# Seven block products for two of eight pairs of tiles in the values, the gates and both output projections, and a later first such pair in w2

## The chip, the cores and the metric

The kernel runs on one core of a Trainium2 chip. The metric is the device time of one execution in microseconds (us); the kernel before has a median of 1559.32 us over 3 runs (1559.26 to 1560.52). Five engines work side by side, each through its own list of instructions in order: TensorE (PE, matrix products), VectorE (DVE), ScalarE (ACT), GpSimd (POOL) and SyncE (SP, which issues the transfers from memory).

## The reference

One decoder layer on 256 tokens of width 2048, in fp32. Matrices that the change touches: the three column groups of `w_in` that give values and gates, `w_out`, and `xo`, all multiplied by a 256-row operand, and `w2`, whose plan alone changes.

```python
proj = x @ w_in[l]
q_m, k_m, v_m, o_m, i_m, f_m, q_a, k_a, v_a = split_columns(proj, IN_SPLITS)
y_m = mlstm_mixer(q_m, k_m, v_m, o_m, i_m, f_m, conv_w[l], conv_b[l], gate_b[l], mh_g[l])
y_a = dilated_attention(q_a, k_a, v_a, rel_bias)
x = layer_norm(ALPHA * x + concat(y_m, y_a) @ w_out[l], ln_g[l, 0], ln_b[l, 0])
y = memory_cross_attention(x, mem, xq[l], xk[l], xv[l], xo[l])      # ends in o @ xo
x = layer_norm(ALPHA * x + y, ln_g[l, 1], ln_b[l, 1])
x = layer_norm(ALPHA * x + (silu(x @ w1[l]) * (x @ w3[l])) @ w2[l], ln_g[l, 2], ln_b[l, 2])
```

## The kernel before

**Split products.** TensorE multiplies fp32r numbers. To keep fp32 accuracy every operand is kept as a high and a low part, and each product of tiles is three matmuls: high by high, high by low, low by high. A matmul takes a 128x128 stationary tile of the operand and 512 columns of the weights.

**The way of the weights.** Weights come from memory as raw tiles `w` of 1 MB, which hold a *pair* of k-tiles (two times 128 rows, 1024 columns); a ring of 3 such tiles (RAW). ACT casts a k-tile to its high part (`h`), DVE subtracts it from the raw tile to get the low part (`l`); a ring of 5 such couples (SPLIT). Then PE uses both.

**The plain product** (`gemm_tokens`) goes through 8 pairs, that is 16 k-tiles, for 2 halves of 128 rows and 2 column halves: 16 x 2 x 2 x 3 = 192 matmuls into 4 banks of PSUM. The values `v0`, `v1`, the gates `v2`, the halves of the first output projection `wo0`, `wo1` and of the second one `xo0`, `xo1` are done so, `f0` too. After `v0` and `v1`, `rows_of` copies the 4 banks to SBUF (2 copies on ACT, 2 on DVE); after `v2` ACT takes the tanh straight from the banks; after the projections `Norm.add` scales the residual `z` and adds the banks.

**The product with sevens** (`gemm_seven`) is used before for the groups `f2` to `f20` of the feed-forward block and for `w2` (`w2a0`, `w2a1`, `w2b0`, `w2b1`). A plan lists the pairs; one in brackets is a *seven*: its 2x2 blocks (two k-tiles, two column halves, two row halves) are multiplied in a scheme of seven block products `P1`, `P2`, `P3`, `Q4`, `P5`, `P7`, `Q6` in place of eight, so 21 matmuls in place of 24. For it, `sums` adds the raw weights on DVE (L308, one instruction over 128x1024, L312 and L313 over 128x512), and the weights, the sums included, are split in one piece of 512 and three of 1024 columns. The operand's tiles must be mixed too (`mix_again`: L152, four adds L141 to L144, and a split). The results lie in 5 banks of the pool `pg` (P1, P2, P3, Q4, E) and 3 of the pool `ps` (P5, P7, Q6), which is all of PSUM; once the last seven is done, `early` combines P1, P5, P7 and Q6 with `z` (`into_z`, 1 copy on ACT and 7 instructions on DVE) or with rows in SBUF (`into_rows`, 1 copy and 4 instructions); when the last plain pair is done the other four banks are added.

**The order.** Each engine's list is laid out ahead by a scheduler that simulates the kernel; so instructions of one stage stand among those of others. Around `v1` DVE's list has the convolution of the queries and keys (L583, L588, L594) and the attention (L495 to L506); around `w2a0` the end of `f10`, whose products of the gate (silu on ACT L953, products on DVE L954) are turned by PE (L959, tile `f10p`) and split into `hT`; after `xo1` the second normalization (L663, L713 to L731), whose rows PE turns for `f0` (L742, tile `x2p`). `xo1` keeps its last 6 k-tiles (LAG) in SBUF and does their products with the second row half at the end, so that the first row half can go through the normalization meanwhile.

Of the kernel before, what the change touches and what calls it, by code (L numbers as in the profile page):

```python
# [50 lines left out]
def decoder_layer(ctx: ExitStack, tc: tile.TileContext, A):  # L51
# [360 lines left out]

    def rows_of(banks, name):
        out = []
        for m in range(2):
            out.append([slot(f"{name}{m}{c}") for c in range(2)])
            for c in range(2):
                (SC.copy if c else V.tensor_copy)(out[m][c], banks[m][c])
        return out

    def turned(rows, j, name):
# [692 lines left out]
```

## Time and profile before

| | us |
|---|---|
| median of 3 runs | 1559.32 |
| the profiled execution's own time | 1558.89 |
| its span in the trace | 1557.0 |
| PE busy | 1533.5 |
| DVE busy | 1097.5 |
| ACT busy | 753.0 |

The span is the time from the first to the last instruction of the trace. Busy times of PE come from modelled ends of pipelined matmuls. The engine letters are those of the first section; PEclk is the clock that was granted to TensorE in a stretch, as a share of the full 2.4 GHz.

### The profile page before, as it was taken

To read this page: it belongs to the slowest core of one execution; us is meant where nothing else is said; L and a number is where in the kernel's file an instruction comes from. 1 tells how busy PE (TensorE), PEld (TensorE's weight loads), DVE (VectorE), ACT (ScalarE), POOL (GpSimd) and SP (SyncE) were. 2 spreads that over 40 slices of the span, in tenths; PEclk is the share of its full clock that TensorE was granted. 3 is DMA by queue.
4 is the path that set the end of the run, shared out by engine and by line. 5 is a ranking of instruction groups with operands and counts; after the bars stand their busy time and mean duration, and the time that the engine had idled before them with its cause. 6 is when DMAs were issued, how large, how long until landed. Compare 5 with 4: busy or idle time off the path is not lost.

```text
span 1557.0 us, 19142 instructions
## 1 busy us (share of the span) xinstructions
PE 1533.5 (98%) x7452; PEld 1284.9 (83%) x7452; DVE 1097.5 (70%) x1426; ACT 753.0 (48%) x974; POOL 28.3 (2%) x30
## 2 busy tenths in 40 slices
PE   9999999999999999999998999999899999999997
PEld 7888888888888888888887888887788888888885
DVE  6555774586557655555559678887788778888997
ACT  5445554454433544444434554555446455555551
POOL 0000000000000000000004000000000000000000
PEclk9999999999999999999999999999999999999999
DMA  8664455575554555445553465665465656667552
GB/s 300 238 237 176 150 196 190 185 263 184 200 193 163 201 187 196 180 139 192 188 189 135 163 214 192 216 193 191 147 222 177 205 189 192 214 192 258 199 189 108
DMA packets 83352, 301.33 MB, mean 194 GB/s; under 512 B 7181, under 2 KB 9402, under 8 KB 59710
## 3 DMA queue, kind: packets, MB, share of 16 engines
q1 hardware_dynamic: 83262, 300.12, 56.0%
q8 instruction: 58, 0.95, 0.2%
q14 instruction: 32, 0.26, 0.1%
HBM read 297.97 MB, written 4.21 MB: 194 GB/s over the span
## 4 chain that ended last, share of the span: by engine, by line
PE 96%; DVE 3%; DMA 1%; issue 0%; ACT 0%; SPq 0%; DVEq 0%; ACTq 0%
PE w2a0P L338 2%; PE w2a1P L338 2%; PE w2b0P L338 2%; PE w2b1P L338 2%; PE f10P L338 2%; PE f18P L338 1%; PE f16P L338 1%; PE f14P L338 1%; PE f20P L338 1%; PE f8P L338 1%; PE f12P L338 1%; PE f2P L338 1%; PE f6P L338 1%; PE f4P L338 1%; PE w2a0Q L338 1%; PE w2a1Q L338 1%
## 5 line engine op out<-in xcount | busy, mean ns | idle before, releaser
L257 DVE TENSOR_TENSOR v2l<-v2w,v2h 128x1024 fp32r<-128x1024 f32 x16 | 19.6, 1225 | 21.9 <-ACT v2h L256 21.9
L257 DVE TENSOR_TENSOR v0l<-v0w,v0h 128x1024 fp32r<-128x1024 f32 x16 | 19.6, 1226 | 21.7 <-ACT v0h L256 21.6
L257 DVE TENSOR_TENSOR xv1l<-xv1w,xv1h 128x1024 fp32r<-128x1024 f32 x16 | 19.6, 1225 | 20.7 <-ACT xv1h L256 20.6
L257 DVE TENSOR_TENSOR xv0l<-xv0w,xv0h 128x1024 fp32r<-128x1024 f32 x16 | 19.6, 1226 | 19.9 <-ACT xv0h L256 19.9
L257 DVE TENSOR_TENSOR wo0l<-wo0w,wo0h 128x1024 fp32r<-128x1024 f32 x16 | 19.6, 1226 | 18.7 <-ACT wo0h L256 18.5
L110 ACT CAST w2a1h<-w2a1w 128x1024 fp32r<-128x1024 f32 (+1 forms) x24 | 22.8, 981 | 20.4 <-PE w2a1E L338 11.8
L257 DVE TENSOR_TENSOR xo0l<-xo0w,xo0h 128x1024 fp32r<-128x1024 f32 x16 | 19.6, 1225 | 18.4 <-ACT xo0h L256 18.4
L257 DVE TENSOR_TENSOR wo1l<-wo1w,wo1h 128x1024 fp32r<-128x1024 f32 x16 | 19.4, 1223 | 17.9 <-ACT wo1h L256 17.7
L110 ACT CAST w2a0h<-w2a0w 128x1024 fp32r<-128x1024 f32 (+1 forms) x24 | 22.7, 979 | 16.8 <-PE w2a0E L338 8.2
L256 ACT CAST wo1h<-wo1w 128x1024 fp32r<-128x1024 f32 x16 | 16.8, 1055 | 26.7 <-PE wo1b L276 18.4
L256 ACT CAST f0h<-f0w 128x512 fp32r<-128x512 f32 (+1 forms) x22 | 16.8, 813 | 26.5 <-PE xo1b L276 14.5
L256 ACT CAST v2h<-v2w 128x1024 fp32r<-128x1024 f32 x16 | 16.9, 1055 | 25.2 <-PE v2b L276 18.5
L257 DVE TENSOR_TENSOR v1l<-v1w,v1h 128x1024 fp32r<-128x1024 f32 x16 | 19.6, 1223 | 13.1 <-ACT v1h L256 13.1
L256 ACT CAST v0h<-v0w 128x1024 fp32r<-128x1024 f32 x16 | 16.9, 1054 | 24.6 <-PE v0b L276 19.4
L256 ACT CAST xv1h<-xv1w 128x1024 fp32r<-128x1024 f32 x16 | 16.9, 1055 | 23.8 <-PE xv1b L276 17.2
L111 DVE TENSOR_TENSOR w2a1l<-w2a1w,w2a1h 128x1024 fp32r<-128x1024 f32 (+1 forms) x24 | 26.5, 1130 | 2.5 <-ACT w2a1h L110 2.5
L110 ACT CAST w2b0h<-w2b0w 128x1024 fp32r<-128x1024 f32 (+1 forms) x20 | 19.2, 988 | 17.0 <-PE w2b0E L338 10.1
L256 ACT CAST xv0h<-xv0w 128x1024 fp32r<-128x1024 f32 x16 | 16.9, 1054 | 21.6 <-PE xv0b L276 16.4
L256 ACT CAST wo0h<-wo0w 128x1024 fp32r<-128x1024 f32 x16 | 16.9, 1054 | 21.3 <-PE wo0b L276 15.0
L111 DVE TENSOR_TENSOR w2a0l<-w2a0w,w2a0h 128x1024 fp32r<-128x1024 f32 (+1 forms) x24 | 26.4, 1129 | 0.9 <-ACT w2a0h L110 0.9
L338 PE MATMUL w2a0P<-w2a0h,hT 128*128 128x512 f32 x80 | 26.8, 395 | 0.0
L256 ACT CAST xo0h<-xo0w 128x1024 fp32r<-128x1024 f32 x16 | 16.8, 1051 | 20.4 <-PE xo0b L276 16.2
(1388 smaller groups left out, 5431.6 us busy)
## 6 DMA issues: line engine op xcount, KB each, us to landing
w2a0w<-in_w SPq DMA_DIRECT2D x12, 1024.0 KB, 5.0
w2a1w<-in_w SPq DMA_DIRECT2D x12, 1024.0 KB, 4.9
w2b0w<-in_w SPq DMA_DIRECT2D x10, 1024.0 KB, 5.0
w2b1w<-in_w SPq DMA_DIRECT2D x10, 1024.0 KB, 4.9
v0w<-in_w_v SPq DMA_DIRECT2D x8, 1024.0 KB, 5.1
v1w<-in_w_v SPq DMA_DIRECT2D x8, 1024.0 KB, 4.9
v2w<-in_w_v SPq DMA_DIRECT2D x8, 1024.0 KB, 4.9
wo0w<-in_w_out SPq DMA_DIRECT2D x8, 1024.0 KB, 4.9
```

The costliest lines, as they stand in the source:

```text
L110: SC.copy(hi, src)
L111: V.tensor_tensor(out=lo, in0=src, in1=as_f32(hi), op=ALU.subtract)
L256: SC.copy(wh[:, cs], w[:, i, cs])
L257: eng.tensor_tensor(out=wl[:, cs], in0=w[:, i, cs], in1=as_f32(wh[:, cs]), op=ALU.subtract)
L338: T.matmul(of[to], lhsT, rhs, start=to not in begun, stop=end)
```

## The change

`v0`, `v1`, `v2`, `wo0`, `wo1`, `xo0` and `xo1` go from `gemm_tokens` to `gemm_seven`, each with 2 sevens among its 8 pairs; operand pairs 2 and 5 of `xT`, 5 and 7 of `yT`, 1 and 3 of `oT` are mixed once for it. `rows_of` is gone; `whole` (4 adds on DVE) adds the last banks to the rows of `into_rows`, and the tanh of the gates reads those rows. The plan of `w2a0` and `w2a1` keeps its four sevens (pairs 2, 4, 6, 8), but three plain pairs stand ahead of the first one where one did.

```diff
-    def rows_of(banks, name):
...
-                (SC.copy if c else V.tensor_copy)(out[m][c], banks[m][c])
+    def whole(rows, banks):
+        for m in range(2):
+            for c in range(2):
+                V.tensor_tensor(out=rows[m][c], in0=rows[m][c], in1=banks[m][c], op=ALU.add)
...
     def in_rows(i):
-        return gemm_tokens(xT, A["w_v"][i], KT, f"v{i}")
+        rows, plan = [], [0, 1, (2,), 3, 4, (5,), 6, 7]
+        if not xT.mixed:
+            xT.mix_again(2)
+            xT.mix_again(5)
+        banks = gemm_seven(xT, fetch(A["w_v"][i], f"v{i}"), KT, f"v{i}", plan, into_rows(rows, f"v{i}r"))
+        whole(rows, banks)
+        return rows
...
-    va = rows_of(in_rows(0), "va")
+    va = in_rows(0)
...
-    vm = rows_of(in_rows(1), "vm")
+    vm = in_rows(1)
...
-    banks = in_rows(2)
+    gate = in_rows(2)
...
-            SC.activation(t, banks[m][c], ACT.Tanh, scale=0.5)
+            t = gate[m][c]
+            SC.activation(t, t, ACT.Tanh, scale=0.5)
...
+    for j in (5, 7):
+        yT.mix_again(j)
     for g in range(2):
-        banks = gemm_tokens(yT, A["w_out"][g], KT, f"wo{g}", order, last=g == 1)
+        get, plan = fetch(A["w_out"][g], f"wo{g}"), [0, 2, (1,), 4, 5, (3,), 6, 7]
+        banks = gemm_seven(yT, get, KT, f"wo{g}", plan, into_z(g, ALPHA), order, last=g == 1)
         for m in range(2):
-            ln.add(m, g, banks, stats=False)
+            ln.add(m, g, banks, stats=False, scale=1.0)
...
-    banks = gemm_tokens(oT, A["xo"][0], KT, "xo0")
+    for j in (1, 3):
+        oT.mix_again(j)
+    plan = [0, 2, (1,), 4, (3,), 5, 6, 7]
+    banks = gemm_seven(oT, fetch(A["xo"][0], "xo0"), KT, "xo0", plan, into_z(0, ALPHA))
...
-    banks = gemm_tokens(oT, A["xo"][1], KT, "xo1", kept=range(KT - LAG, KT), last=True)
+    plan, kept = [0, (1,), 2, (3,), 4, 5, 6, 7], range(KT - LAG, KT)
+    banks = gemm_seven(oT, fetch(A["xo"][1], "xo1"), KT, "xo1", plan, into_z(1, ALPHA), None, kept, True)
...
     def w2_first():
-        plan = [0, (2,), 1, (4,), 3, (6,), 5, (8,), 7, 9, 10, 11]
+        plan = [0, 1, 3, (2,), 5, (4,), 7, (6,), 9, (8,), 10, 11]
```

In the lists of instructions that follow, the number behind a name's letters is that of its pair or k-tile, and the one behind the underscore tells tiles of one name apart.

DVE's list before, where `f10` ends and `w2a0` begins: the products of `f10`'s gate (L954), the split of `hT` from the turned tile `f10p`, and the sums of the first two sevens, pairs 2 and 4.

```order
L954 TENSOR_TENSOR f10ru_8795<-f10ru_8795,f10r00_8796 128x256
L954 TENSOR_TENSOR f10r11_8798<-f10r11_8798,f10r00_8796 128x256
L954 TENSOR_TENSOR f10r01_8797<-f10r01_8797 128x256
L111 TENSOR_TENSOR hT10_8887<-f10p0_8882,hT10_8887 128x2x256
L308 TENSOR_TENSOR w2a0t2_8947<-w2a0w2_8945 128x1024
L308 TENSOR_TENSOR w2a0t4_9025<-w2a0w4_9023 128x1024
L111 TENSOR_TENSOR hT11_8900<-f10p1_8895,hT11_8900 128x2x256
L312 TENSOR_TENSOR w2a0s2_8948<-w2a0t2_8947,w2a0w2_8945 128x512
```

The same place of DVE's list now (the gate's products are at L962):

```order
L111 TENSOR_TENSOR w2a0l6_9261<-w2a0w3_9258,w2a0h6_9260 128x1024
L962 TENSOR_TENSOR f10ru_9074<-f10ru_9074,f10r00_9075 128x256
L962 TENSOR_TENSOR f10r11_9077<-f10r11_9077,f10r00_9075 128x256
L111 TENSOR_TENSOR w2a0l7_9277<-w2a0w3_9258,w2a0h7_9276 128x1024
L111 TENSOR_TENSOR w2a0l2_9300<-w2a0w2_9292,w2a0h2_9299 128x512
L962 TENSOR_TENSOR f10r01_9076<-f10r01_9076 128x256
L111 TENSOR_TENSOR hT10_9166<-f10p0_9161,hT10_9166 128x2x256
L111 TENSOR_TENSOR w2a0l2_9307<-w2a0w2_9292,w2a0h2_9306 128x1024
L308 TENSOR_TENSOR w2a0t2_9294<-w2a0w2_9292 128x1024
L308 TENSOR_TENSOR w2a0t4_9372<-w2a0w4_9370 128x1024
L111 TENSOR_TENSOR hT11_9179<-f10p1_9174,hT11_9179 128x2x256
L312 TENSOR_TENSOR w2a0s2_9295<-w2a0t2_9294,w2a0w2_9292 128x512
```

The splits of pair 3 (and ahead of these, those of pair 1) now stand among the gate's products; the sums still follow the last of these products, and PE has three plain pairs to do ahead of the first seven.

DVE's list before in the middle of `v1`, at the end of the convolution (L588, L594) and the start of an attention head (L495):

```order
L257 TENSOR_TENSOR v1l5_1946<-v1w2_1927,v1h5_1945 128x1024
L588 SCALAR_TENSOR_TENSOR k0_1842<-q0_1639,cw_535,k0_1842 128x254
L257 TENSOR_TENSOR v1l6_1964<-v1w3_1961,v1h6_1963 128x1024
L594 SCALAR_TENSOR_TENSOR i5r1_1828<-i5r1_1828,i4r1_1625 128x512
L588 SCALAR_TENSOR_TENSOR k0_1842<-q0_1639,cw_535,k0_1842 128x253
L257 TENSOR_TENSOR v1l7_1980<-v1w3_1961,v1h7_1979 128x1024
L495 SCALAR_TENSOR_TENSOR i2r0_1088<-sc7_1425,tb4_523 128x384
```

The same place of DVE's list now (the convolution's lines are L580 and L586, the head's is L487); `v1l2` are the weights of the first seven, pair 2, and `v1l6` those of the k-tile that follows it:

```order
L111 TENSOR_TENSOR v1l2_1993<-v1w2_1978,v1h2_1992 128x1024
L580 SCALAR_TENSOR_TENSOR k0_1889<-q0_1686,cw_535,k0_1889 128x253
L111 TENSOR_TENSOR v1l2_2003<-v1t2_1980,v1h2_2002 128x1024
L586 SCALAR_TENSOR_TENSOR i5r1_1875<-i5r1_1875,i4r1_1672 128x512
L111 TENSOR_TENSOR v1l2_2013<-v1s2_1981,v1h2_2012 128x1024
L586 SCALAR_TENSOR_TENSOR i4r1_1672<-k0_1889 128x512
L487 SCALAR_TENSOR_TENSOR i2r0_1135<-sc7_1472,tb4_523 128x384
L308 TENSOR_TENSOR v1t5_2092<-v1w5_2090 128x1024
L111 TENSOR_TENSOR v1l6_2025<-v1w3_2022,v1h6_2024 128x1024
```

Three splits of the seven stand where two plain ones stood, and the sum of the second seven (`v1t5`), which needs its raw tile, stands ahead of the split of the next plain k-tile.

PE's list now at the same seven (`xT2` is the plain operand, `xTm2` the mixed one):

```order
L338 MATMUL v1P1_1906<-v1h2_1985,xT2_156 128x512
L338 MATMUL v1P1_1906<-v1l2_1986,xT2_156 128x512
...
L338 MATMUL v1Q4_1904<-v1h2_2012,xT2_156 128x512
L338 MATMUL v1Q4_1904<-v1l2_2013,xT2_156 128x512
L338 MATMUL v1Q4_1904<-v1h2_2012,xT2_156 128x512
L338 MATMUL v1P2_1902<-v1h6_2024,xT3_183 128x512
L338 MATMUL v1P3_1903<-v1h6_2024,xT3_183 128x512
L338 MATMUL v1Q4_1904<-v1h6_2024,xT3_183 128x512
L338 MATMUL v1E_1905<-v1h6_2024,xT3_183 128x512
L338 MATMUL v1P2_1902<-v1l6_2025,xT3_183 128x512
```

P1, P2, P3 and Q4 of the seven (12 matmuls) are followed at once by the plain k-tile; its P5, P7 and Q6, whose banks of `ps` the attention holds, come later in the list.

## Rows read from the trace of the kernel before

**Rows 1.** The page of the profile: busy time of the engines, its share of the span, and their instructions.

```profile
PE 1533.5 (98%) x7452; PEld 1284.9 (83%) x7452; DVE 1097.5 (70%) x1426; ACT 753.0 (48%) x974; POOL 28.3 (2%) x30
```

**Rows 2.** The chain that ended last, in order of time: start, length in us, and the matmuls of a stretch in which PE waited for nothing. The first is of the group `f4`, a product with sevens, the second of the last product.

```profile
919.37 5.44 PE f4P L338 x24
...
1524.82 10.88 PE w2b1P L338 x48
```

**Rows 3.** Busy time in stretches of the span, from the first matmul of a product to that of the next. By row: v0, v1, v2, wo0, wo1, xo0 (with the last attention head into the memory inside), xo1, f0, f4, w2a0, w2a1. Columns: from and to, length, then busy us and instructions of PE, PEld, DVE, ACT, POOL, then PEclk, share of the DMA engines, GB/s.

```profile
52.70:97.00 44.30, 44.30 (x195) 35.72 (x194) 19.23 (x19) 16.68 (x17) 0.00 (x0) 1.00 0.77 264
204.20:250.50 46.30, 46.30 (x212) 38.39 (x211) 30.76 (x47) 21.90 (x29) 0.00 (x0) 1.00 0.58 198
250.50:294.90 44.40, 44.40 (x201) 36.84 (x200) 21.03 (x19) 18.61 (x20) 0.00 (x0) 1.00 0.55 190
398.30:441.80 43.50, 43.50 (x194) 36.01 (x193) 22.85 (x23) 18.97 (x21) 0.00 (x0) 1.00 0.56 194
441.80:485.50 43.70, 43.70 (x194) 36.20 (x193) 24.36 (x26) 16.86 (x17) 0.00 (x0) 1.00 0.55 193
729.50:779.40 49.90, 49.90 (x247) 42.21 (x245) 25.54 (x30) 20.82 (x26) 0.00 (x0) 1.00 0.52 183
779.40:823.10 43.70, 43.70 (x195) 36.17 (x194) 27.39 (x40) 17.31 (x27) 6.19 (x5) 1.00 0.46 168
823.10:876.00 52.90, 48.25 (x224) 38.97 (x223) 43.03 (x60) 24.20 (x38) 13.93 (x10) 1.00 0.51 179
919.00:962.50 43.50, 43.50 (x197) 36.03 (x196) 36.80 (x48) 23.33 (x29) 0.00 (x0) 1.00 0.60 195
1092.80:1163.50 70.70, 66.50 (x286) 53.57 (x285) 57.17 (x66) 33.59 (x38) 0.00 (x0) 0.95 0.51 178
1163.50:1226.10 62.60, 62.60 (x278) 51.86 (x277) 52.41 (x57) 31.99 (x33) 0.00 (x0) 1.00 0.58 202
```

**Rows 4.** The same view inside `w2a0`, the two stretches around its first seven.

```profile
1098.00:1104.70 6.70, 3.62 (x20) 2.54 (x18) 3.46 (x5) 2.52 (x4) 0.00 (x0) 0.92 0.00 0
1104.70:1111.00 6.30, 5.18 (x12) 3.25 (x13) 6.27 (x8) 3.35 (x4) 0.00 (x0) 0.55 0.35 114
```

**Rows 5.** What PE waited for over the whole span: engine and tile that wait, what they wait for, us in total, times, longest.

```profile
PE w2a0P L338 <- ACT w2a0h L110: 2.5, 1, 2.5
...
PE f0b L273 <- DVE f0l L257: 2.1, 2, 1.6
PE f0b L276 <- DVE x L111: 1.8, 1, 1.8
```

**Rows 6.** DVE at the end of `f10` and the start of `w2a0` in order of time: start us, length us, instruction, and in brackets the idle time before it with what ended it.

```profile
1101.19 0.43 DVE L954 TENSOR_TENSOR f10r<-f10r 128x256 f32<-128x256 f32 x1 [5.15 <-ACT f10r L953]
...
1102.28 2.35 DVE L308 TENSOR_TENSOR w2a0t<-w2a0w 128x1024 f32<-128x1024 f32 x2
```

**Rows 7.** PE at the same place: two turns of `f10`'s rows, and the second matmul of the first seven.

```profile
1101.84 0.27 PE L959 MATMUL f10p<-ident,f10ru 128*128 128x128 f32 x1
1101.95 0.27 PE L959 MATMUL f10p<-ident,f10r 128*128 128x128 f32 x1
...
1107.01 0.80 PE L338 MATMUL w2a0P<-w2a0l,hTm 128*128 128x512 f32 x1 [1.12 <-DVE w2a0l L111]
```

**Rows 8.** Groups of DVE instructions by line and shape in the stretch that holds `f4`: busy us, mean ns of one, idle before. L111 over 1024 and 512 columns are splits, L308, L312 and L313 the sums of raw weights, L694 one step of `into_rows`.

```profile
L111 DVE TENSOR_TENSOR f4l<-f4w,f4h 128x1024 fp32r<-128x1024 f32 x14 | 16.9, 1219 | 4.3 <-ACT f4h L110 4.3
...
L308 DVE TENSOR_TENSOR f4t<-f4w 128x1024 f32<-128x1024 f32 x2 | 2.4, 1222 | 2.3 <-DMA f4w<-in_w 2.3
...
L111 DVE TENSOR_TENSOR f4l<-f4w,f4h 128x512 fp32r<-128x512 f32 x2 | 1.4, 684 | 0.0
L312 DVE TENSOR_TENSOR f4s<-f4t,f4w 128x512 f32<-128x512 f32 x2 | 1.4, 682 | 0.0
L313 DVE TENSOR_TENSOR f4s<-f4s,f4w 128x512 f32<-128x512 f32 x2 | 1.4, 682 | 0.0
...
L694 DVE TENSOR_TENSOR f4r<-f4ru,f4P 128x512 f32<-128x512 f32 x1 | 0.7, 677 | 0.0
```

**Rows 9.** The mixing of one operand pair for the feed-forward block, by the tile `x2r`: durations in ns (lowest, median, highest) and start in us. L141 is the first of four alike.

```profile
L152 DVE TENSOR_TENSOR x2r<-x x1: 693/693/693, 849.3 to 849.3; 128x512 f32<-128x512 f32 x1
L141 DVE TENSOR_TENSOR x2r<-x2r x1: 285/285/285, 850.5 to 850.5; 128x128 f32<-128x128 f32 x1
...
L111 DVE TENSOR_TENSOR x2m<-x2r,x2m x1: 691/691/691, 852.3 to 852.3; 128x512 fp32r<-128x512 f32 x1
```

**Rows 10.** DVE inside `v1`: busy time of a stretch (columns as in rows 3).

```profile
203.10:222.10 19.00, 19.00 (x91) 15.82 (x90) 18.88 (x40) 10.74 (x18) 0.00 (x0) 1.00 0.57 192
```

**Rows 11.** DVE inside `v1` in order of time: the first operation on a bank of `i5`, the product ahead of `v1`, and a split in the middle of the convolution.

```profile
203.18 0.40 DVE L408 TENSOR_TENSOR q<-i5b,i4r 128x256 f32<-128x256 f32 x1
...
211.91 1.22 DVE L257 TENSOR_TENSOR v1l<-v1w,v1h 128x1024 fp32r<-128x1024 f32 x1
```

**Rows 12.** PE inside `v1`: the last instruction of an attention head's scores; 7 matmuls of the first 4 k-tiles are still to come behind it.

```profile
214.99 0.38 PE L493 MATMUL sc<-i3r,i2r 128*128 128x128 f32 x2
```

**Rows 13.** Transfers of raw weights for `v1`, from the page: issues, KB each, median us from issue to landing.

```profile
v1w<-in_w_v SPq DMA_DIRECT2D x8, 1024.0 KB, 4.9
```

**Rows 14.** DVE at the end of `xo1`: the first row half's way through the second normalization.

```profile
814.73 1.28 DVE L663 SCALAR_TENSOR_TENSOR z<-z,xo1b 128x512 f32<-128x512 f32 x2 [11.11 <-PE xo1b L276]
...
821.53 1.19 DVE L731 SCALAR_TENSOR_TENSOR xk1r<-xk1r,l1r,l1g 128x512 f32<-128x512 f32 x1
```

More of the change, by code (lines that the diff above doesn't have):

```diff
@@ L411, in features @@
         return out
-    def rows_of(banks, name):
[L414 to L417, printed above, removed]
-                (SC.copy if c else V.tensor_copy)(out[m][c], banks[m][c])
-        return out
     def turned(rows, j, name):
@@ L808, in decoder_layer @@
         V.tensor_scalar(out=t, in0=t, scalar1=0.5, scalar2=None, op0=ALU.mult)
-    banks = in_rows(2)
-    gate = [[None] * 2 for _ in range(2)]
+    gate = in_rows(2)
     for m in range(2):
         for c in range(2):
-            t = slot(f"gate{m}{c}")
-            SC.activation(t, banks[m][c], ACT.Tanh, scale=0.5)
+            t = gate[m][c]
+            SC.activation(t, t, ACT.Tanh, scale=0.5)
             V.scalar_tensor_tensor(out=t, in0=t, scalar=1.0, in1=mg[c], op0=ALU.add, op1=ALU.mult)
-            gate[m][c] = t
     free(*mg)
@@ L930, in decoder_layer @@
     ln = Norm(1, "l1")
-    banks = gemm_tokens(oT, A["xo"][0], KT, "xo0")
+    for j in (1, 3):
+        oT.mix_again(j)
+    plan = [0, 2, (1,), 4, (3,), 5, 6, 7]
+    banks = gemm_seven(oT, fetch(A["xo"][0], "xo0"), KT, "xo0", plan, into_z(0, ALPHA))
     for m in range(2):
-        ln.add(m, 0, banks)
-    banks = gemm_tokens(oT, A["xo"][1], KT, "xo1", kept=range(KT - LAG, KT), last=True)
+        ln.add(m, 0, banks, scale=1.0)
+    plan, kept = [0, (1,), 2, (3,), 4, 5, 6, 7], range(KT - LAG, KT)
+    banks = gemm_seven(oT, fetch(A["xo"][1], "xo1"), KT, "xo1", plan, into_z(1, ALPHA), None, kept, True)
     x2 = Operand("x2")
     for m in range(2):
-        ln.add(m, 1, banks)
+        ln.add(m, 1, banks, scale=1.0)
         ln.finish(m)
@@ L991, in decoder_layer @@
         banks = gemm_seven(x2, get, KT, f"f{g}", plan, into_rows(rows, f"f{g}r"), last=g == n - 2)
-        for m in range(2):
-            for c in range(2):
-                V.tensor_tensor(out=rows[m][c], in0=rows[m][c], in1=banks[m][c], op=ALU.add)
+        whole(rows, banks)
         hidden(g, rows, lambda b, i: [b[i][:, x * 256 : (x + 1) * 256] for x in range(2)], f"f{g}")
```

## The prediction

> **What bounds the kernel now.** First the busy times: PE 1533.5 of 1557.0 us [rows 1], so 23.5 us is all that PE idles, and DVE (1097.5) and ACT (753.0) have room on average. An average says nothing of a stage, so next the chain that ended last: in the plain stretches it is matmuls alone, 24 in 5.44 us and 48 in 10.88 [rows 2], 0.2267 us each. Then the table by stage [rows 3]: in the seven products that the change touches PE is busy all the time (v0 44.30 of 44.30, xo1 43.70 of 43.70), so there a matmul less is 0.2267 us less, as long as PE's inputs keep up. Two stages show idle PE: w2a0 (66.50 of 70.70) and f0 (48.25 of 52.90), with the waits that go with them [rows 5].
>
> **Matmuls removed.** A seven is 21 matmuls in place of 24, so 2 sevens in 7 products remove 2 x 7 x 3 = 42: 42 x 0.2267 = 9.5 us. The w2 plan keeps its count. That this spacing holds in a product with sevens is shown by f4: 43.50 us at the full clock with none idle [rows 3], its plain pair at 0.2267 each [rows 2]. The Trainium skill (TensorE: Matmul & The Clock Gate, "Wait — 56ns, not 53.3ns?") gives a warm spacing of N / 2.4 GHz + 2.5 ns, 215.7 ns at 512 columns. By that price the term would be 9.1 us; the measured spacing, 226.7 ns, decides.
>
> **w2a0.** Before, its first seven follows one plain pair. DVE's list has the sums of that seven behind the last product of f10's gate, which starts at 1101.19 after 5.15 us of waiting for ACT; the sums start at 1102.28 [rows 6], and the second matmul of the seven at 1107.01 [rows 7], 14.2 us after the stage began at 1092.80. PE idles 4.2 us there in all, and then runs slow: the granted clock is 0.92 from 1098.0 to 1104.7 and 0.55 from 1104.7 to 1111.0 [rows 4], which is mostly the lower of its two levels, 1.2 GHz. w2a1 does the same 276 matmuls in 62.60 us, none idle, clock 1.00 [rows 3]. Eight turns of f10's rows, 0.11 us apart [rows 7], stand in w2a0 alone: 0.9 us. So the loss is 70.70 - 62.60 - 0.9 = 7.2 us. Now three plain pairs stand ahead of the seven: 72 x 0.2267 + 0.9 = 17.2 us, 3 more than the 14.2 after which the weights came. The order shows two things in DVE's way. The splits of pair 3 now stand among the gate's products, and they have their data early, so that costs only their own time. And the sum of the next seven (pair 4) still stands directly behind that of pair 2, ahead of the split of `hT11` and of the first seven's later weights; it needs the raw tile of pair 4, whose buffer is pair 3's. That buffer is free when pair 3's second split is done, for which I take 5 to 9 us into the stage (behind the gate's silu on ACT), and with 4.9 us of transfer (other weights of the same size, [rows 13]) the data is there at 10 to 14, the sums done by 16, the first seven's third weights by 17.5 or so; PE wants them at 17.2 + 9 x 0.2267 = 19.2. I take the whole 7.2 us as gained; bounds: 3.0 (the clock alone, if the wait is the same 4.2 elsewhere) and 8.1 (the turns hidden too).
>
> **What DVE gets.** Per seven: sums of 1.22 + 0.68 + 0.68 = 2.6 us, and splits of 0.68 + 3 x 1.22 in place of 2 x 1.22, 1.9 more [rows 8]. Per product two of these, 9.0, and the combining: 4 instructions of `into_rows` and 4 of `whole` at 0.68 less the 2 copies of `rows_of` (taken at 0.68 too), 4.1; or 7 of `into_z`, 4.8. So 13.1 to 13.8 us. The mixing costs 0.69 + 4 x 0.29 + 0.69 = 2.5 us a pair [rows 9], six times, in v0, wo0 and xo0. Against the stages, each 1.4 us shorter: v0 19.2 + 13.1 + 5.0 = 37.3 of 42.9; wo1 24.4 + 13.8 = 38.2 of 42.3; xo0 25.5 + 13.8 + 5.0 = 44.3 of 48.5; xo1 27.4 + 13.8 = 41.2 of 42.3; v1 30.8 + 13.1 = 43.9 of 44.9 [rows 3]. f4 has 36.80 of 43.50 and no idle PE: most of the new stages lie at that level, and their work on DVE is hidden by PE's. xo1 and v1 lie above it, and each is followed by hand.
>
> **v1.** DVE is full from 203.10 to 222.10, 18.88 of 19.00 [rows 10], with the convolution and the attention. PE: the scores end at 215.1 [rows 12], 7 matmuls later, at 216.7, the first seven begins. By the new order its first four products are followed at once by the next k-tile, whose low part `v1l6` is wanted by the 17th matmul, at 220.3. DVE: from 203.18 to 211.91 [rows 11] its list loses a split of 1.22 (done earlier now), gains one of 512 columns and one step of the convolution, so the seven's second split runs from about 211.8 to 213.1. That frees the raw tile for pair 5, which lands 4.9 us later [rows 13], at 218.0; its sum, which stands ahead of `v1l6`, takes 1.22 and that split 1.22: 220.5. So 0.2 us late. I take 0.5; bounds 0 and 4 (a transfer that lands two or three us late puts all of it on PE, since everything behind the sum on DVE waits with it).
>
> **xo1 to f0.** The first half of the rows must be normalized while the second half's matmuls run. Before, that begins with 36 matmuls to go; in the new list the last matmul of the first half (P3) has 27 behind it: 2.0 us less cover. DVE's way from 814.73 to the end of the first normalized piece, 821.53 + 1.19 = 822.72 [rows 14], is 8.0 us. Two of its adds and sums of statistics now go with P2 ahead of P3, some 1.3 us less. I take 0.7 us lost. Bounds: a gain of 1 (f0's waits of 2.1 and 1.8 [rows 5] shrink) and a loss of 3 (DVE is late by then: its 11.11 us of waiting [rows 14] are what the 13.8 are put into).
>
> **The rest.** A product with sevens holds all 5 banks of `pg`, and the next finds only that of P1 free when it starts (a plain one holds 4, and one is spare); f4 follows f2 and w2a1 follows w2a0 in that way without idle PE [rows 3], so the nearest rows say 0. The starts that differ from these (v0 behind i1, attention and keys behind these products, mixing ahead of v0, wo0, xo0) have no row: 0 to 1 us each, and I take 1.5 for all seven. wo0 has the mLSTM's last head among its first matmuls and wo1 comes behind it while `into_z` is on DVE: 0.8 (0 to 3).
>
> **Sum,** against the profiled execution's 1558.89 us: -9.5 - 7.2 + 0.5 + 0.7 + 1.5 + 0.8 = -13.2, so 1545.7; the median lies 0.43 above that execution: 1546.1, given as 1546.0.
>
> **Rivals.**
> (a) All is hidden: -9.5 - 7.2 = -16.7, 1542.6 against the median. For it: f4's row. Against it: v1 and xo1 above 97% of DVE.
> (b) DVE becomes the bound in the dense stages. f0 has DVE at 43.03 of 52.90 and 4.65 us idle PE [rows 3], because what PE wants comes last in a row on DVE. If two or three of v1, wo0, xo1 lose so: -16.7 + 9.3 to 14.0, 1552 to 1556.6. Against it: PE's and DVE's lists were laid out with these sums in them, and the hand work finds v1 within 0.5.
> (c) The stall of w2a0 moves only: the 4.2 us return at the second seven or at the sum of pair 4, which keeps its place on DVE; the low clock with them. Then -9.5 + 3.5 for the rest: 1553.3.
> (d) **Slower.** Sevens whose weights come late make PE wait, and TensorE's clock falls behind each such wait, as in w2a0: 7.2 us a place, idle time and 0.55 of the clock [rows 4]. In v1's first seven, at wo0/wo1, and behind xo1 the conditions are alike (sums on DVE behind a chain that waits). From three places on, 21.6 us, it outweighs 16.7 by more than can be measured: 1564. Against it: f0's waits of 1.8 and 2.1 did not slow the clock (1.00 in its row). The Trainium skill (same page, "The HAM clock gate") says the halved clock is the default and activity lifts it; [rows 4], where it falls behind the wait, agree.
>
> **Chances.** Forecast 0.56 (1543.5 to 1551), (a) 0.12, (b) 0.14, (c) 0.08, (d) 0.10. A measurement of this kernel tells 0.2% from no change, 3.1 us: faster is below 1556.2. Forecast, (a), most of (b) and (c) are faster: 0.56 + 0.12 + 0.10 + 0.06 = 0.84; within 0.2%: 0.04 + 0.02 + 0.02 of (d) = 0.08; slower 0.08. The range takes in (a) with the gain of 1 us that xo1 may bring, 1541.5, and (c) and most of (b) above, 1555.5; outside are (d) and the top of (b).
>
> **What the new profile would show.** PE busy falls by some 9.5 plus the slow matmuls of w2a0 (3 us); w2a0 takes 63 to 64 us at clock 1.00; each of the seven products takes 1.36 us less (v0 near 42.9, wo1 near 42.3), DVE 33 to 38 us busy in v0 and wo1. Waits of PE on `v1l`, on `x2p` or `f0b` above 2 us would show rival (b), a clock below 0.9 in one of the new stages (d), a wait on `w2a0t` or `w2a0l` (c). The prediction is wrong above all if DVE is late in xo1 or v1 by more than the hand work says.

## The result and the profile after

The changed kernel takes 1546.55 us (median of 4 runs, 1546.24 to 1548.75) against 1559.92 us before (4 runs, 1559.26 to 1560.52): a ratio of 0.9917, 95% interval 0.99 to 0.9935, so 13.4 us or 0.8% less. Forecast were 1546.0 us and a range of 1541.5 to 1555.5. The profiled execution took 1546.63 us, with a span of 1544.8: 12.2 us less in the trace.

The page of the profile after, busy time of the engines; it answers to [rows 1]:

```profile
PE 1526.1 (99%) x7410; PEld 1277.2 (83%) x7410; DVE 1192.9 (77%) x1584; ACT 775.7 (50%) x1011; POOL 30.9 (2%) x30
```

PE works 7.4 us less and idles 18.7 us of the span (before 23.5). Some 12.5 us less work were forecast; matmuls at the low clock count as busy, and there are new ones behind xo1 (below). DVE has 95 us more to do, ACT 23 us. PE stays the bound.

Stretches of the span from the first matmul of a product to that of the next, columns as in [rows 3]: v0, v1, v2, wo0 (from its second matmul; the first stands alone at 389.3, among those of the product ahead), wo1, xo0, xo1 up to its last matmuls, f0 with the end of xo1's normalization, f4, w2a0, w2a1.

```profile
52.50:94.90 42.40, 42.40 (x186) 34.16 (x185) 27.76 (x32) 18.67 (x21) 0.00 (x0) 1.00 0.76 260
202.60:247.60 45.00, 45.00 (x206) 37.33 (x205) 38.44 (x60) 24.03 (x32) 0.00 (x0) 1.00 0.53 187
247.60:290.00 42.40, 42.40 (x189) 35.12 (x188) 32.68 (x36) 21.03 (x23) 0.00 (x0) 1.00 0.63 228
394.80:436.60 41.80, 41.80 (x186) 34.59 (x185) 36.40 (x44) 22.66 (x27) 0.00 (x0) 1.00 0.60 218
436.60:478.80 42.20, 42.20 (x188) 34.94 (x187) 36.57 (x44) 20.00 (x22) 0.00 (x0) 1.00 0.56 199
723.20:771.60 48.40, 48.40 (x240) 40.96 (x239) 36.95 (x47) 23.43 (x31) 0.00 (x0) 1.00 0.54 192
771.60:815.00 43.40, 42.45 (x187) 34.66 (x186) 38.41 (x53) 22.09 (x34) 8.12 (x6) 1.00 0.50 175
815.00:868.40 53.40, 50.72 (x224) 40.97 (x225) 43.37 (x62) 23.66 (x36) 13.80 (x9) 0.94 0.51 177
911.50:955.00 43.50, 43.50 (x197) 36.02 (x196) 36.55 (x47) 23.33 (x29) 0.00 (x0) 1.00 0.61 194
1085.10:1150.40 65.30, 64.45 (x286) 52.31 (x285) 54.07 (x63) 33.44 (x38) 0.00 (x0) 1.00 0.54 194
1150.40:1213.00 62.60, 62.60 (x278) 51.84 (x277) 51.39 (x56) 31.37 (x33) 0.00 (x0) 1.00 0.58 201
```

In v0, v1, v2, wo0, wo1 and xo0 PE is busy in all of the stretch at clock 1.00, as before; DVE's 36.40 of 41.80 in wo0 is the densest of them. Idle PE is found behind xo1 (42.45 of 43.40, then 50.72 of 53.40, with the clock at 0.94) and in w2a0 (64.45 of 65.30, clock 1.00, before 0.95).

What PE waited for, all rows above 0.3 us:

```profile
PE x2p L739 <- DVE xk1r L728: 2.3, 2, 1.3
PE pw L435 <- POOL idle L433: 1.5, 1, 1.5
PE i0b L392 <- ACT i0h L256: 1.2, 2, 0.8
PE x2p L739 <- DVE z L728: 0.9, 1, 0.9
PE w2a0Q L338 <- ACT w2a0h L110: 0.5, 1, 0.5
PE f0b L276 <- DVE x L111: 0.4, 1, 0.4
PE f10Q L338 <- ACT f10h L110: 0.4, 1, 0.4
```

No row names v0 to xo1's weights: none of the new sevens' splits came late. The waits on `w2a0h` fell from 2.5 us [rows 5] to 0.5. At the start of f0 those on `f0b` fell from 3.9 [rows 5] to 0.4, but those on `x2p` (the turn of the normalized rows; the rows `xk1r` and `z`) rose from 0.6 to 3.2. Over xo1 and f0 together PE idles 3.6 us now (0.95 and 2.68) and idled 4.7 before: less, not more; what is new there is the low clock.

By the first matmul of each product in the two traces, the 12.2 us come from these stretches (a plus is a loss; i2 to v1, 106.2 in both, is left out):

| from the first matmul of ... to that of ... | before, us | after, us | difference |
|---|---|---|---|
| the start to v0 | 52.7 | 52.5 | -0.2 |
| v0 to i2 (the product behind it) | 45.3 | 43.9 | -1.4 |
| v1 to v2 | 46.4 | 45.0 | -1.4 |
| v2 to i6 | 44.8 | 43.4 | -1.4 |
| i6 to wo1 (wo0 lies in it) | 146.5 | 145.6 | -0.9 |
| wo1 to xk2 | 43.5 | 42.2 | -1.4 |
| xk2 to xo0 | 244.2 | 244.4 | +0.2 |
| xo0 to xo1 | 49.9 | 48.5 | -1.4 |
| xo1 to f2 (f0 lies in it) | 96.7 | 96.8 | 0 |
| f2 to w2a0 | 216.7 | 216.7 | 0 |
| w2a0 to w2a1 | 70.6 | 65.3 | -5.3 |
| w2a1 to f14 | 104.7 | 104.7 | 0 |
| f14 to f20 | 129.4 | 130.1 | +0.7 |
| f20 to the end | 159.4 | 159.6 | +0.2 |

Differences are taken before rounding. Five products have their 1.36 us (6 matmuls of 0.2267), to within 0.03; the stretch that holds wo0 has 0.9; the seventh, xo1, has nothing left of it when f2 begins; and w2a0 gives 5.3.

### The profile page after: what moved, and what is told of

It is laid out like the page before. It is cut to its first block, busy times and chain, and to the rows that moved or that the text cites. A ratio compares the mean times of both kernels' runs of the same rounds, so it can differ in the third digit from the quotient of the medians.

```text
span 1544.8 us, 19283 instructions
## 1 busy us (share of the span) xinstructions
PE 1526.1 (99%) x7410; PEld 1277.2 (83%) x7410; DVE 1192.9 (77%) x1584; ACT 775.7 (50%) x1011; POOL 30.9 (2%) x30
## 4 chain that ended last, share of the span: by engine, by line
PE 95%; DVE 3%; DMA 1%; issue 1%; ACT 0%; SPq 0%; DVEq 0%; ACTq 0%
PE w2a1P L338 2%; PE w2a0P L338 2%; PE w2b0P L338 2%; PE w2b1P L338 2%; PE f10P L338 2%; PE f20P L338 2%; PE v1P L338 2%; PE xo0P L338 2%; PE xo1P L338 2%; PE v0P L338 1%; PE f18P L338 1%; PE f8P L338 1%; PE wo0P L338 1%; PE f4P L338 1%; PE f2P L338 1%; PE f6P L338 1%
## 5 line engine op out<-in xcount | busy, mean ns | idle before, releaser
L257 DVE TENSOR_TENSOR xv1l<-xv1w,xv1h 128x1024 fp32r<-128x1024 f32 x16 | 19.6, 1224 | 20.7 <-ACT xv1h L256 20.6
L257 DVE TENSOR_TENSOR xv0l<-xv0w,xv0h 128x1024 fp32r<-128x1024 f32 x16 | 19.6, 1225 | 20.0 <-ACT xv0h L256 20.0
L111 DVE TENSOR_TENSOR w2a0l<-w2a0w,w2a0h 128x1024 fp32r<-128x1024 f32 (+1 forms) x24 | 26.5, 1131 | 6.1 <-ACT w2a0h L110 6.1
L111 DVE TENSOR_TENSOR w2a1l<-w2a1w,w2a1h 128x1024 fp32r<-128x1024 f32 (+1 forms) x24 | 26.4, 1131 | 5.6 <-ACT w2a1h L110 5.6
L257 POOL TENSOR_TENSOR f0l<-f0w,f0h 128x512 fp32r<-128x512 f32 x12 | 20.0, 1696 | 314.6 <-ACT f0h L256 314.6
L110 ACT CAST w2b1h<-w2b1w 128x512 fp32r<-128x512 f32 (+1 forms) x28 | 19.8, 758 | 12.5 <-PE w2b0E L338 5.4
L338 PE MATMUL w2a1P<-w2a1h,hT 128*128 128x512 f32 x80 | 25.4, 389 | 0.0
L110 ACT CAST wo1h<-wo1w 128x1024 fp32r<-128x1024 f32 (+1 forms) x16 | 15.6, 1000 | 18.9 <-PE wo1E L338 11.3
L110 ACT CAST f12h<-f12w 128x1024 fp32r<-128x1024 f32 (+1 forms) x16 | 15.6, 1000 | 18.7 <-PE f12E L338 11.3
L273 PE MATMUL f0b<-f0l,x 128*128 128x512 f32 x64 | 24.9, 405 | 0.1
L273 PE MATMUL xv0b<-xv0l,mT 128*128 128x512 f32 x64 | 25.0, 391 | 0.0
L111 DVE TENSOR_TENSOR w2b0l<-w2b0w,w2b0h 128x1024 fp32r<-128x1024 f32 (+1 forms) x20 | 22.2, 1139 | 3.6 <-ACT w2b0h L110 3.6
L272 PE MATMUL xv1b<-xv1h,mT 128*128 128x512 f32 x64 | 24.9, 392 | 0.0
L272 PE MATMUL xv0b<-xv0h,mT 128*128 128x512 f32 x64 | 24.9, 389 | 0.0
L273 PE MATMUL xv1b<-xv1l,mT 128*128 128x512 f32 x64 | 24.9, 389 | 0.0
L272 PE MATMUL f0b<-f0h,x 128*128 128x512 f32 x64 | 24.7, 407 | 0.0
```

The costliest lines, as they stand in the source:

```text
L110: SC.copy(hi, src)
L111: V.tensor_tensor(out=lo, in0=src, in1=as_f32(hi), op=ALU.subtract)
L257: eng.tensor_tensor(out=wl[:, cs], in0=w[:, i, cs], in1=as_f32(wh[:, cs]), op=ALU.subtract)
L272: T.matmul(banks[m][c], xh, wh[:, cs], start=n == 0, stop=False)
L273: T.matmul(banks[m][c], xh, wl[:, cs], start=False, stop=False)
L338: T.matmul(of[to], lhsT, rhs, start=to not in begun, stop=end)
```

## The experiments

All ran against the kernel before, on one chip for each set; where runs of several sets bear on each other, the difference to the kernel before is compared.

**The two halves alone.** One kernel takes only the new plan of w2, the other everything but that:

```diff
-        plan = [0, (2,), 1, (4,), 3, (6,), 5, (8,), 7, 9, 10, 11]
+        plan = [0, 1, 3, (2,), 5, (4,), 7, (6,), 9, (8,), 10, 11]
```

> The kernel before with the new plan of w2 alone (three plain pairs ahead of the first seven), everything else as before. Theory (the stall at the start of w2a0 is a matter of where its first seven stands, and is cured without the new sevens): 5.3 us faster than before, as w2a0 became shorter in the trace of the change (70.7 to 65.3), so near 1554.6, and the granted clock of w2a0 is 1.00. Rival (the stall went because the whole program's list was laid out anew by the sevens, the plan has little to do with it): within 1 us of before, and the dip to about 0.55 stays.

> The change without the new plan of w2: sevens in the seven products, w2's plan as before. Theory (the parts add up): 13.4 less 5.3, so 8.1 us faster than before, near 1551.8, with w2a0 still near 70.7 us and a dip of the clock there. Rival (DVE-bound: the sevens bring little, the plan brings most): within 3 us of before. Rival (w2a0's stall goes by the new layout): near the changed kernel, 1546.5.

Measured: 1553.77 us against 1559.75 for the plan alone (ratio 0.9962, 0.9948 to 0.9976: 6.0 us) and 1552.78 for the sevens alone (0.9957, 0.9945 to 0.997: 7.0 us). Together 13.0; both at once gave 13.4. So the parts add up, and w2a0's stall is a matter of the place of its first seven: with the old plan PE's wait of 2.5 us on `w2a0h` is there again, in the kernel with all the new sevens as in that without.

```profile
PE w2a0P L338 <- ACT w2a0h L110: 2.5, 1, 2.5
...
PE w2a0P L338 <- DVE w2a0l L111: 1.6, 1, 1.6
```

**The sevens by groups.** The kernel before with `gemm_seven` in v0, v1 and v2 alone, in wo0 and wo1 alone, and in xo0 and xo1 alone. Each takes its part of the diff of the change.

> The kernel before with sevens in v0, v1 and v2 alone. Theory (each matmul left out is 0.2267 us, all of DVE's new work is hidden): 18 matmuls, 4.1 us faster, near 1555.8. Rival (v1, where DVE has 98% by the sum, holds PE up): 2 us faster or less, with waits of PE on v1l.

> The kernel before with sevens in wo0 and wo1 alone. Theory: 12 matmuls, 2.7 us, less the 0.3 that the trace of the change shows lost around them: 2.4 faster, near 1557.5. Rival (the mLSTM's last head and the combining into z between wo0 and wo1 hold PE up): 1 us faster or less.

> The kernel before with sevens in xo0 and xo1 alone. Theory (12 matmuls are 2.7 us, of which 1.4 are given back at the start of f0, where the normalization has less cover): 1.3 us faster, near 1558.6, with PE waiting for x2p 2 to 3 us. Rival (DVE, at 97% by the sum, is late all through xo1): PE waits on xo1l, and it is no faster than before. Rival (nothing is given back): 2.7 faster.

Measured: v 1556.1 us against 1559.75 (ratio 0.9977, 0.9967 to 0.9986: 3.7 us); wo 1556.84 (0.9982, 0.9973 to 0.9991: 2.9 us); xo 1558.61 against 1559.51 (0.9996, 0.9987 to 1.0004: 0.9 us, inside the interval of no difference). For v and wo that is near the price of the matmuls, 4.1 and 2.7. For xo it is a third of 2.7. Its trace has 48.5 us from xo0 to xo1 (before 49.9), and 97.3 from xo1 to f2 (before 96.7), with the waits of PE on `x2p` that the changed kernel has (3.3 us). So xo0 pays and xo1 does not.

**The price of a matmul with DVE's work left in.** Each new seven repeats one low product of P1 three times, so that it has the 24 matmuls of a plain pair and all of the new work on DVE and ACT:

```diff
+                    if to == "P1" and name[:2] in ("v0", "v1", "v2", "wo", "xo"):
+                        for _ in range(3):
+                            product(to, xl, wh[:, cs], False)
```

> The changed kernel, in which each of the 14 new sevens does 3 matmuls more: the low-by-high product of its P1 is done four times in place of once, so its result differs. All of the new work on DVE and ACT stays. Theory (the gain is PE's matmuls alone, DVE's work is hidden): 42 x 0.2267 = 9.5 us slower than the changed kernel, near 1556.1. Rival (the stages are bound by DVE in part): the added matmuls find PE idle, and it is 6 us slower or less.

Measured: 1554.46 us against 1559.51 (ratio 0.9966, 0.9954 to 0.9979), 5.05 us faster than before, so 8.3 us slower than the changed kernel (13.4). It lies between the two numbers expected, and the stretch from xo1 to f2 says why:

```profile
780.20:876.90 96.70, 93.67 (x418) 76.39 (x417) 82.48 (x114) 45.63 (x69) 20.96 (x14) 0.98 0.50 176
```

96.70 us with 6 matmuls more, where the changed kernel has 96.8 and the kernel before 96.7. The first matmul of xo1 stands at 780.2 here, 8.6 us later than in the changed kernel, 0.3 of them from the start. So 36 matmuls of six products cost 8.3 us, 0.23 each: PE bound them, and DVE's new work there is covered. The 6 of xo1 cost nothing: with them PE idles 3.0 us from xo1 to f2 where the changed kernel idles 3.6, and the clock is 0.98 where it is 0.96.

**xo1 without sevens** (with four plain pairs ahead of w2's first seven, see below):

```diff
-    plan, kept = [0, (1,), 2, (3,), 4, 5, 6, 7], range(KT - LAG, KT)
-    banks = gemm_seven(oT, fetch(A["xo"][1], "xo1"), KT, "xo1", plan, into_z(1, ALPHA), None, kept, True)
+    banks = gemm_tokens(oT, A["xo"][1], KT, "xo1", kept=range(KT - LAG, KT), last=True)
```

> The kernel with four plain pairs ahead of w2's first seven, and with xo1 as before, without sevens (xo0 keeps its two). Theory (six matmuls more in xo1 cost nothing, since PE waits for the normalization behind it for as long; six of the seven products pay in full): within 0.6 us of the kernel with four plain pairs, 1545.2 to 1546.4. Rival (a matmul is 0.2267 us there too): 1.4 us slower, 1547.2.

Measured: 1546.04 us (ratio to the kernel before 0.9912, 0.9899 to 0.9926), 13.6 us less than the kernel before, where the kernel that differs by xo1 alone has 13.75: 0.1 us apart, where six matmuls are 1.36. It confirms what the row above says. From xo1 to f2, the three kernels before, after and this one:

```profile
779.40:876.10 96.70, 92.05 (x417) 75.22 (x416) 70.47 (x99) 41.61 (x64) 20.13 (x14) 1.00 0.49 174
771.60:868.40 96.80, 93.17 (x411) 75.62 (x411) 81.79 (x114) 45.76 (x69) 21.92 (x14) 0.96 0.50 176
772.70:869.50 96.80, 92.16 (x418) 75.28 (x417) 69.84 (x99) 41.63 (x64) 20.12 (x14) 1.00 0.49 174
```

With its sevens xo1 lets PE idle 1 us less, but PE is busy 1 us more, at the lower clock. In the profiles of all eight kernels that have sevens in xo1 the clock fell in this stretch (0.95 to 0.98 over it), in none of the six without (1.00).

**What delays f0.** DVE after, at the end of xo1, in order of time; it answers to [rows 14]:

```profile
807.97 0.69 DVE L655 SCALAR_TENSOR_TENSOR z<-z,xo1P 128x512 f32<-128x512 f32 x1 [0.40 <-PE xo1P L338]
...
811.11 2.46 DVE L723 SCALAR_TENSOR_TENSOR z<-z,l1mv,l1g 128x512 f32<-128x512 f32 x2
813.49 0.68 DVE L655 SCALAR_TENSOR_TENSOR z<-z,xo1Q 128x512 f32<-128x512 f32 x1
814.08 2.85 DVE L728 SCALAR_TENSOR_TENSOR xk1r<-xk1r,l1r,l1g 128x512 f32<-128x512 f32 x2
816.86 3.43 DVE L728 SCALAR_TENSOR_TENSOR z<-z,l1r,l1b 128x512 f32<-128x512 f32 x2
```

The last bank of the first row half comes at 807.97. The rows of two instructions of L723 and L728 come to 1.2, 1.4 and 1.7 us an instruction, where the same kind takes 0.7 to 0.75 in quiet stretches; L655, which reads a bank of PSUM, takes 0.68 among them. PE waits three times for these rows:

```profile
815.31 0.66 PE L739 MATMUL x2p<-ident,xk1r 128*128 128x128 f32 x4 [1.26 <-DVE xk1r L728]
816.99 0.80 PE L739 MATMUL x2p<-ident,xk1r 128*128 128x128 f32 x4 [1.03 <-DVE xk1r L728]
818.67 1.12 PE L739 MATMUL x2p<-ident,z 128*128 128x128 f32 x4 [0.88 <-DVE z L728]
```

From 811.45 on GpSimd computes low parts of f0's weights:

```profile
811.45 16.39 POOL L257 TENSOR_TENSOR f0l<-f0w,f0h 128x512 fp32r<-128x512 f32 x10 [0.53 <-ACT f0h L256]
```

Before, that run of ten began at 820.42 with the end of xo1 at 822.9, so it slowed only the last normalizing instructions. The Trainium skill (SBUF — State Buffer, "Who interferes with whom") says that a DVE instruction with two inputs in SBUF contends with a GpSimd instruction that reads SBUF, since its second input comes through a read port that the two share, and that one with a single SBUF input, outside the modes that use two ports, does not. The rows agree: L723 and L728 read two tiles of SBUF and are slowed, L655 reads one and is not. Two kernels try to mend it. The first keeps two k-tiles more of xo1 for the end:

```diff
-LAG, HEAD, LAG2 = 6, 6, 8
+LAG, HEAD, LAG2 = 8, 6, 8
```

> The changed kernel, but xo1 keeps its last 8 k-tiles (LAG 8, before 6), so that 48 and not 36 matmuls of the second row half are put off to the end. Theory (what f0 loses is cover for the first row half's normalization): the waits on x2p (3.2 us) and the dip of the clock behind them go, 1 to 2.5 us faster than the changed kernel, 1544 to 1545.5. Rival (the normalization is late because GpSimd's splits for f0 slow DVE, whatever the cover): the waits stay, within 0.5 us of the changed kernel.

Measured: 1553.84 us against 1559.51 (ratio 0.9962, 0.9949 to 0.9976), 7.7 us slower than the changed kernel: a miss for both theories. The waits on `x2p` did shrink, from 3.2 to 0.5 us, but one of 9.0 came:

```profile
PE f0b L276 <- DVE x L111: 9.0, 1, 9.0
...
PE x2p L739 <- DVE z L728: 0.5, 1, 0.5
```

DVE there, from 820.91 on: the second row half's normalization stands ahead of the split of the first `x` in its list.

```profile
821.27 3.49 DVE L723 SCALAR_TENSOR_TENSOR z<-z,l1mv,xe 128x512 f32<-128x512 f32 x2
824.68 3.41 DVE L723 SCALAR_TENSOR_TENSOR z<-z,l1mv,l1g 128x512 f32<-128x512 f32 x2
828.02 1.07 DVE L111 TENSOR_TENSOR x<-x2p,x 128x256 fp32r<-128x256 f32 x3
```

The list was laid out anew with the larger LAG, and four instructions of 1.7 us, slowed by GpSimd, now run between the turned rows and their split. PE had nothing else to do, and its granted clock fell to 0.50 between 824 and 829. The second kernel takes f0's low parts from GpSimd to DVE:

```diff
-                eng = G if at in kept and kept[0] == 0 else V
+                eng = V
```

> The changed kernel, but the low parts of f0's first 6 k-tiles are computed on DVE, not on GpSimd. Theory (what f0 loses at its start is DVE being slowed while GpSimd works: an instruction of 128x512 takes 1.2 to 1.7 us there and 0.68 elsewhere): DVE's normalization goes back to 0.7 us an instruction, PE's waits on x2p (3.2 us) and the dip of the clock shrink, 1 to 3 us faster than the changed kernel, 1543.5 to 1545.5. Rival (the chain is late because it has less cover, and 12 splits more on DVE, 8.2 us, come on top): the waits grow, 2 us or more slower.

Measured: 1549.24 us against 1559.66 (ratio 0.9935, 0.9923 to 0.9947), 2.9 us slower than the changed kernel, as the rival said. Yet the cause that the theory named is there: with GpSimd quiet the normalization is back at 0.75 us an instruction, and the waits on `x2p` fall to 0.6. But the moved splits stand ahead of the split of `x` and PE waits 5.4 us for that. DVE there:

```profile
815.08 0.75 DVE L728 SCALAR_TENSOR_TENSOR xk1r<-xk1r,l1r,l1g 128x512 f32<-128x512 f32 x1
...
820.67 3.09 DVE L257 TENSOR_TENSOR f0l<-f0w,f0h 128x512 fp32r<-128x512 f32 x5
823.68 1.08 DVE L111 TENSOR_TENSOR x<-x2p,x 128x256 fp32r<-128x256 f32 x3
```

So the slowing by GpSimd is shown, and that taking it away pays is not: in both kernels what f0's start costs is decided by what stands ahead of the split of `x` on DVE.

**One plain pair more ahead of the first seven** of w2a0 and w2a1, in the changed kernel:

```diff
-        plan = [0, 1, 3, (2,), 5, (4,), 7, (6,), 9, (8,), 10, 11]
+        plan = [0, 1, 3, 5, (2,), 7, (4,), 9, (6,), 10, (8,), 11]
```

> The changed kernel with one plain pair more (four) ahead of the first seven of w2a0 and w2a1. Theory (w2a0 still loses some 1.8 us because the sums wait until f10's rows are turned, then come just too late): w2a0 becomes 64 us or less, 0.8 to 1.8 us faster than the changed kernel. Rival (what is left in w2a0 is not the order but the turns themselves and their gaps): within 0.5 us of it.

Measured: 1545.76 us against 1559.51 (ratio 0.9911, 0.9897 to 0.9924), 0.4 us more gained than by the change (13.75 against 13.4), and its median is 0.8 lower. No row of PE's waits names w2a0 any more. That is the direction of the theory; the size is inside what repeats of one kernel differ by. In the traces, from w2a0's first matmul to f14's, it takes 168.8 us where the changed kernel takes 170.0.

**The slots.** DVE in the changed kernel, where w2a0's first seven is prepared; it answers to [rows 6]:

```profile
1095.12 0.42 DVE L962 TENSOR_TENSOR f10r<-f10r 128x256 f32<-128x256 f32 x1
...
1100.43 2.36 DVE L308 TENSOR_TENSOR w2a0t<-w2a0w 128x1024 f32<-128x1024 f32 x2 [2.64 <-PE f10p L967]
```

The sums do not wait for the gate's last product any more (1095.12), but 2.64 us for PE to turn f10's rows: a sum's tile takes the slot of such a row. A last pair of kernels has one slot of SBUF more, for which the small gate weights move into a slot:

```diff
-NSLOT, RAW, SPLIT = 34, 3, 5
+NSLOT, RAW, SPLIT = 35, 3, 5
...
-    gw2 = const.tile([P, KT, 40], F32R, tag="gw2", name="gw2")
+    gw2_t = big("gw2")
+    gw2 = gw2_t[:, : KT * 40].rearrange("p (k c) -> p k c", k=KT)
...
     es, least_norm = gates()
+    free(gw2_t)
```

> The kernel before with its old plans and one SBUF slot more for rows, sums and operands (35 slots, before 34; the room is made by keeping the small gate weights in a slot). In DVE's list the sums of w2a0's first two sevens now stand ahead of the last product of f10's gate and of the split of hT, where before they stood behind both. Theory (the stall of w2a0 came from the sums' place and from slots that f10's rows still held, since their tile was free only when PE had turned the rows): the sums start near 1096, w2a0's waits shrink from 4.2 us to 2 or less and the clock stays up, 4 to 6 us faster than before, 1554 to 1556, without any change of plan. Rival (the first seven simply comes too soon after f10 for DVE, whatever the slots): within 1.5 us of before.

> The changed kernel with the same slot more. Theory: the sums of w2a0's first seven, which wait 2.64 us for f10's turned rows in the changed kernel, no longer do, and PE's last idle time there (0.85 us) goes: 0.5 to 1.8 us faster than the changed kernel. Rival (the rest of w2a0's loss is the turns themselves): within 0.5 us of it.

Measured, with the old plans: 1557.27 us against 1559.59 (ratio 0.9983, 0.9974 to 0.9991), 2.3 us faster, half of what the theory said and more than the rival's. The profiled execution, 1556.01, is among the faster of 11 (1555.99 to 1557.50). One of the two sums ran at 1095.25, the other still waited for the turn; PE idles 3.9 us in w2a0 (before 4.2), so the waits did not shrink to 2, but the clock stayed at 1.00 (before 0.95):

```profile
1095.25 1.23 DVE L308 TENSOR_TENSOR w2a0t<-w2a0w 128x1024 f32<-128x1024 f32 x1
1100.01 1.23 DVE L308 TENSOR_TENSOR w2a0t<-w2a0w 128x1024 f32<-128x1024 f32 x1 [3.54 <-PE f10p L961]
...
1092.00:1160.70 68.70, 64.84 (x286) 52.32 (x285) 57.05 (x66) 33.46 (x38) 0.00 (x0) 1.00 0.52 184
```

In the changed kernel: 1546.26 us against 1559.59 (0.9921, 0.9908 to 0.9935), no different from it as a whole. By stretches it is: w2a0 takes 63.60 us, none idle, as long as w2a1 and the turns together (62.60 and 0.9),

```profile
1086.80:1150.40 63.60, 63.60 (x285) 52.46 (x284) 54.06 (x63) 33.46 (x38) 0.00 (x0) 1.00 0.55 199
```

and from f10's first matmul to w2a0's it is 43.1 us where it was 44.3. But from xo1 to f2 it is 99.3 us where it was 96.8, with waits of 2.8 and 1.2 us on `x2p` and 1.2 on `f0b`: PE's list came out otherwise there (four matmuls of f0 now stand ahead of the last turn of the first row half). Most of a local gain of 2.9 us went to another stage whose code is the same.

## Why the prediction was right, and where its terms were off

The sum forecast -13.2 us on the profiled execution; 12.3 were measured (1558.89 to 1546.63). Term by term:

- **Matmuls removed, -9.5.** Right for six products: the six stretches that hold them give 7.8 (8.2 by the spacing, less 0.5 around wo0), and 36 repeated matmuls cost 8.3 there. An estimate by the Trainium skill's spacing (TensorE: Matmul & The Clock Gate, "Wait — 56ns, not 53.3ns?"), 215.7 ns, gives 7.8 for 36; the trace's 226.7 stands nearer to what the repeated ones cost. That DVE's new work would be covered was the main reason, and rival (b) fell with it: no split of a new seven came late, in v1 (0.5 us forecast, 0 found) as elsewhere.
- **xo1 to f0, +0.7.** The direction was right (less cover for the first half's normalization) and the size half of what it was: the stretch from xo1 to f2 is as long as before instead of 1.36 us shorter, so 1.4 went. The step that fell short is DVE's way, taken at its old 8.0 us less 1.3, 6.7. That way was read to the row at 821.53, called the first normalized piece; it is the second, the first stands at 820.27 in the trace before:

```profile
820.27 0.74 DVE L731 SCALAR_TENSOR_TENSOR xk1r<-xk1r,l1r,l1g 128x512 f32<-128x512 f32 x1
```

  To the end of the second piece the way takes 9.0 us now (807.97 to 816.93): three of its instructions run beside GpSimd's splits, at which the prediction did not look, and an add of the second half (813.49) stands among them. PE waits 1.26 and 1.03 us for the two pieces and 0.88 for the third. These waits are not the whole account, since PE idles less than before in all. The first matmul of f0 that needs DVE's split of `x` shows the rest, before and after:

```profile
828.39 0.73 PE L276 MATMUL f0b<-f0h,x 128*128 128x512 f32 x2 [1.83 <-DVE x L111]
...
821.87 1.22 PE L276 MATMUL f0b<-f0h,x 128*128 128x512 f32 x2 [0.38 <-DVE x L111]
```

  It stood 49.0 us behind xo1's first matmul and now stands 50.3 behind it, though six matmuls are gone: 1.3 lost. From there to f2 1.2 us are won: the waits on `f0l`, 2.1 us [rows 5], are gone, but the clock is low until 824. What the low clock alone costs no run shows; up to 821.87 PE would have waited for DVE anyhow, which has no idle time ahead of that split, and of the four executions the one with the highest mean granted clock (0.998, the profiled one 0.995) took 1546.24 us, only 0.4 less than the profiled one.
- **w2a0, -7.2.** It gave 5.3. The stall, the clock and the place of the cure were right (the plan alone gives 6.0 us). What was missing: the prediction counted three plain pairs as 3 us more than needed, but the sums came at 1100.43, 15.3 us into the stage where the working has both done by 16; they were tied to the turn of f10's rows through the slots, so that the seven's later weights were late by 0.5 and 0.2 us, and matmuls around them were spread. With one slot more the stretch is 63.60 us, which is the forecast.
- **The rest, +1.5 and +0.8.** 0.7 was found (0.5 around wo0, 0.2 from xk2 to xo0). The rows that said 0 for the transition between two products with sevens were right, and the allowance beside them was too large.
- **Not foreseen:** +0.7 between f14 and f20, whose code is unchanged. PE idles 0.24 us there (a wait on the row tile of `into_rows`); the rest is open. The kernel with 35 slots has 129.4 us there, as before, so it hangs on the layout and not on the chip.

The errors (+0.7 at xo1, +1.9 at w2a0, +0.7 behind f14, +0.2 behind f20, against -0.5 in v1, -1.6 in the rest and -0.2 at the start) cancel in part, so the closeness of the total, 1 us in the trace, is in part luck. DVE's sums by stage were too high (v0 37.3 forecast and 27.76 found, v1 43.9 and 38.44, wo1 38.2 and 36.57). In part the work fell into the stages beside them: the mixing of xT starts at 11.3 and 21.4, long before v0. In part instructions overlap: those of 0.68 us start 0.60 apart (L668 at 800.88, L670 at 801.48), so DVE's busy time rose by 95 us and not by the 110 that the terms add up to. Rival (c) fell with w2a0's idle PE (0.85 us) and clock (1.00). Two signs did come, both at one place: the waits on `x2p` above 2 us that were to show rival (b), and rival (d)'s low clock, behind late rows and not late weights. It fell to 0.67 and 0.50 around and behind the waits on `x2p`,

```profile
816.00:820.00 4.00, 2.13 (x9) 1.67 (x10) 4.00 (x3) 0.92 (x3) 4.00 (x4) 0.67 0.58 242
820.00:824.00 4.00, 3.62 (x9) 2.40 (x8) 4.00 (x11) 2.35 (x5) 4.00 (x4) 0.50 0.37 102
```

which before it had not done at that place (1.00). One place does not outweigh 16.7 us, as the rival said; the kernel with the larger LAG, with its one wait of 9.0 us, lost 7.7.

## What to carry to other kernels

Where PE is the bound, taking matmuls off it pays in full though DVE gets more to do (here up to 36 of 42 us in a stage), but in a product that stands right ahead of a chain of vector work it can pay nothing: look at what its last matmuls release before counting them. A seven, or anything that needs its inputs prepared, belongs behind enough plain work that the preparation can start after the previous stage has freed its buffers; follow the buffer and not only the list. With a scheduler that lays out every engine's list anew, a change at one end of the program can move 0.7 to 2.5 us at the other (0.7 from f14 to f20, 2.5 from xo1 to f2 with 35 slots), so read gains by stretches and not from the total alone.

## What was not expected of the hardware

While GpSimd ran splits of 128x512 (1.6 us each), DVE's instructions of that size with two inputs in SBUF took 1.2 to 1.7 us on average; with the same splits on DVE they took 0.75. One that began just ahead of a split was not slowed (L257 at 823.82: 1.16 us over 128x1024, in quiet 1.22). Waits of PE of 3.2 us in three pieces came with a granted clock of 0.67 and then 0.50 over 8 us in the changed kernel; 4.7 us of waiting at the same place before, in other pieces, left it at 1.00, and so did 3.9 us in w2a0 of the kernel before with 35 slots, where 4.2 us without the slot had come with 0.55. Each of these is one profiled execution; what decides between them no run here shows.
